# Attention's queries, keys and gates as paired products, and attention's softmax beside branch B's output projection

## The chip, the cores and the metric

One core of a Trainium2 chip runs the whole program. The metric is the device time of one execution in microseconds (us). The kernel before took 1786.78 us, the median of 3 runs (1786.04 to 1786.87).

## The reference

One layer over 512 tokens of width 2048, all in float32. h = RMSNorm(x) goes through one wide projection, whose columns feed two mixers and two merge gates:

```
a_out  = dsa_mixer(aq, ak, av, iq, ik, iw) * silu(az)      # 8 heads x 128, top-k keys by an index score
b_out  = retention_mixer(rope(rq), rope(rk), rv) * silu(rz) # 8 heads x 128, groupnorm
merged = sigmoid(ga) * (a_out @ w_a_out) + sigmoid(gb) * (b_out @ w_b_out)
r      = x + merged @ w_o
out    = rmsnorm(r + (p @ w_ple) * sigmoid(r @ w_ple_gate)) * final_gain
```

Keys that aren't selected get a bias of -1e30 in attention's logits, so attention is computed over all keys up to the query's tile of 128 tokens.

## The kernel before

**Products.** Activations lie transposed: 128 channels on the partitions, 512 tokens along the row. A float32 product is made of three fp32r products: weights and activations are each split in a high part (a ScalarE copy, L137 for weights) and a low part (a subtraction on VectorE or POOL, L143), and TensorE adds high*high, high*low and low*high. `gemm` (L207, matmuls at L197 to L199) does this for one block of 128 output channels: 16 steps over K, three matmuls of 512 columns each.

**Paired products.** `gemm_pair` (L214, matmuls at L249 and L250) makes two output blocks at once from seven half-K products of sums of weight blocks and sums of token halves (a Strassen-like scheme): 7 x 8 steps, each one matmul of 512 and one of 256 columns. It needs the combined inputs `Xh` (56 tiles, made once, kept in DRAM as `hd`, loaded by `x_load`), and its weight sums come from accumulating DMAs on POOL's queue and one VectorE addition (L145). ScalarE copies and VectorE additions (L223, L227, L853) put the outputs together.

**Order.** The order of every engine's instructions is that of the program text. Each K step of a product calls `step()`, which counts a tick and lets side work in: what `later(n, f)` has put n ticks ahead, else the next of the queue `todo`, else, every `rate` ticks, one of the background list `bg`. The background list holds, in this order, the making of `hd`, the top-k rounds on VectorE (L605, L606), and the position bias: four masks on VectorE (L620) and 12 small matmuls (L628) for each of 32 groups, written to `scr` in DRAM. Weights are split 4 units and loaded 9 units ahead of their use, on SP's queue; a unit is 8 K steps of one block.

**Stages.** (1) Index keys and queries with their scores; (2) retention: values (L693 to L695) for four heads, then per head two products `ps_rq` and `ps_rk`, with rotation, scores, states, GroupNorm and a turn back (`turn`, L761) as side work; (3) 22 pairs: branch B's gates, both merge gates and half of attention's gates; (4) branch B's output projection, 16 blocks `ps_w` of 8 steps, with x read again and split in its ticks; (5) attention: values for four heads, then per head the products `ps_aq` and `ps_ak`, and in the ticks of the next head's products the softmax; at its end four more gate products `ps_z` (`gated`); (6) attention's output projection, `ps_w` again from 1327.2 us on; (7) paired products with w_o; (8) the last gate, in 12 blocks and a wider tail.

**Attention of one head.** Logits from split queries and keys (L677 to L679; the first 128 tokens unsplit, L935), added to bias and mask and maximized on VectorE (L937); exponentials with sums on ScalarE (L953); normalization on VectorE (L963, L964); 128 block turns of 32x32 for all heads, 16 a head, on VectorE (`flip`, L708); split into high (L975, ScalarE) and low (L977, VectorE); outputs on TensorE (L989, L991) from split values (L943, L945). The mask is added to the bias on POOL (L916). In this stage and in retention POOL makes the low parts of the weights (`pool_units`).

**Buffers.** 65 slots of 128x512 (`U`), 5 of 128x1280 (`B`), 8 PSUM banks (`P`), 7 raw weight buffers.

Of the kernel before, what the change touches and what calls it, by code (L numbers as in the profile page):

```python
# [34 lines left out]
def block_kernel(tc, xT, pT, posb, posq, w_in, w_v, w_ik, w_a, w_b, w_o, w_ple, w_gate,  # L35
# [4 lines left out]
    with contextlib.ExitStack() as ctx:  # L40
# [265 lines left out]
        for h in range(NH):  # L306
            if h % 4 == 0:
                u_rv.append(block(w_v[h // 4], (2,) * 8, 512))
            if h < NH - 1:
                u_r.append([block(col(g, h), K8) for g in (RQ, RK)])  # L310
            else:
                ids = [block(col(g, h)[:, k:k + 8, :], (8,)) for k in (0, 8) for g in (RQ, RK)]
                u_r.append([ids[0] + ids[2], ids[1] + ids[3]])
        u_rz = [block_pair(col(RZ, h), col(RZ, h + 1)) for h in range(0, NH, 2)]
        u_gb = [block_pair(col(GB, m), col(GB, m + 1)) for m in range(0, 16, 2)]
        u_ga = [block_pair(col(GA, m), col(GA, m + 1)) for m in range(0, 16, 2)]
        u_az = [block_pair(col(AZ, h), col(AZ, h + 1)) for h in range(0, AZ_PAIRED, 2)]
        u_wb = [block(w_b[m], (8,)) for m in range(16)]
        u_a, u_av = [], []
        for h in range(NH):  # L320
            if h % 4 == 0:
                u_av.append(block(w_v[2 + h // 4], (2,) * 8, 512))
            u_a.append([block(col(g, h), K8) for g in (AQ, AK)])
        u_az += [block(col(AZ, h), K8) for h in range(AZ_PAIRED, NH)]
# [5 lines left out]
        pool_units.append((u_a[0][0][0] + 4, u_a[-1][1][-1] + 9))  # L330
# [223 lines left out]
        todo.extend(N3 * 2 + [f_sum] + N3 + [f_rnat] + N3 * 3 + [f_bcast, None, f_keys1] + N3 * 3 + [f_keys2] + N3 * 2 + [f_keys3] + N3 * 2)  # L554
# [127 lines left out]
        def values(ids, name):  # L682
# [3 lines left out]
            for s, (i, k) in enumerate(seq):  # L686
                if k == 0:
                    split_to(i + AHEAD)
                    load_to(i + AHEAD + LOADS)
                h, l = loaded[i]  # L690
                a, b = hparts[s]
                for t in range(NT):
                    pe.matmul(pss[t], a[:, tok(t)], h[:, k], start=(s == 0), stop=False)  # L693
                    pe.matmul(pss[t], a[:, tok(t)], l[:, k], start=False, stop=False)  # L694
                    pe.matmul(pss[t], b[:, tok(t)], h[:, k], start=False, stop=(s == KT - 1))  # L695
                    step()
            vs = [U(name) for _ in range(NT)]
# [4 lines left out]
        def flip(dst, src, n, pairs):  # L702

            d = dst[:, 0:128 * n].rearrange("p (t q) -> p t q", q=128)
            f = src[:, 0:128 * n].rearrange("p (t q) -> p t q", q=128)
            for i in pairs:
                a, b = divmod(i, 4)
                dve.transpose(out=d[32 * a:32 * a + 32, :, 32 * b:32 * b + 32],  # L708
                              in_=f[32 * b:32 * b + 32, :, 32 * a:32 * a + 32])


        yd, bd, zd = (dp.tile([NH, 128, L], F32, name=n) for n in ("yd", "bd", "zd"))
# [11 lines left out]
        def retention_head(h, vs):  # L724
# [4 lines left out]
            if h < NH - 1:  # L729
                pq = gemm(u_r[h][0], hparts, "ps_rq")  # L730
            else:
                i = u_r[h][0][0]
                split_to(i + 4)
                load_to(i + 11)
                x_load(X_AHEAD)
                pq, pk = gemms([(u, slice(0, 128), hparts, ALL, n) for u, n in zip(u_r[h], ("ps_rq", "ps_rk"))],
                               ahead=3, each=lambda s: x_load(2))
            sq = rotate(pq)
            qd = U("qd")
            later(5, lambda: pool.tensor_mul(  # L740
                qd[:, 0:384].rearrange("p (t q) -> p t q", t=3), sq[:, 128:].rearrange("p (t q) -> p t q", t=3),
                dect[:, None, 128:256].to_broadcast([128, 3, 128])))
            if h < NH - 1:
                pk = gemm(u_r[h][1], hparts, "ps_rk")
# [37 lines left out]
            def values_out(t):  # L782
# [6 lines left out]
                if t:  # L789
                    pe.matmul(o, qd[:, tok(t - 1)], E["s"][:, tok(t - 1)], start=False, stop=True)  # L790
# [28 lines left out]
            todo.extend([None] * 5)  # L819
            todo.extend([scores, lambda: keys(0), None, lambda: keys(1)] + [None] * 3 + [states, None, None])  # L820
            todo.extend([lambda t=t: values_out(t) for t in range(NT)])
            todo.extend([None, norm] + [None] * 5 + [scale] + [None] * 5 + [lambda: back(0), None, lambda: back(1)])
# [11 lines left out]
        for h in range(NH):  # L834
            if h % 4 == 0:
                rv = values(u_rv[h // 4], "rv")
            retention_head(h, rv)
        for i in range(len(x_wanted)):
            later(4 + 2 * i, lambda: x_load(1))
        hparts.clear()  # L840
# [5 lines left out]
        def gate_pair(ids, func, finish):  # L846
# [4 lines left out]
            def done(c0, c1, i, q):  # L851
# [3 lines left out]
                if have[i] == 2:  # L855
                    later(1, lambda: (act.activation(o, o, func), finish(i, o)))
# [3 lines left out]
        def to(dst):  # L860
            return lambda i, o: act.dma_start(dst[i], o)

        for n, u in enumerate(u_rz):
            y = B("y2")

            def b_out(i, o, y=y, n=n):
                pool.tensor_mul(o, o, y[:, L * i:L * i + L])
# [7 lines left out]
            gate_pair(u, AF.Silu, b_out)  # L875
        for us, dst in ((u_gb, sgb), (u_ga, sga)):
            for n, u in enumerate(us):
                gate_pair(u, AF.Sigmoid, to(dst[2 * n:2 * n + 2]))
# [6 lines left out]

        for n in range(AZ_PAIRED // 2):
            if n == AZ_PAIRED // 2 - 1:
# [3 lines left out]
            gate_pair(u_az[n], AF.Silu, to(zd[2 * n:2 * n + 2]))  # L891


        def x_again(k):
            xs[k] = U("xk")
            sp.dma_start(xs[k], xT[:, k, :])
            later(5, lambda: x_split(k))

        state["rate"] = 2
        todo.extend([f for k in range(KT) for f in (lambda k=k: x_again(k), None, None, None)])  # L900
        for m in range(16):
            s = U("sg")
            sp.dma_start(s, sgb[m])
            pw = gemm(u_wb[m], bparts, "ps_w")
            dve.tensor_mul(s, pw, s)
            later(4, lambda m=m, s=s: sp.dma_start(mbs[m], s))
        drain()


        oTs = []  # L910

        def attention_head(h, vs):
            hc = slice(128 * (h % 4), 128 * (h % 4) + 128)
            bm = B("bm")
            sp.dma_start(bm, scr[h])
            pool.tensor_add(bm, bm, mneg)  # L916
            ps = gemm(u_a[h][0], hparts, "ps_aq")
            q = U("aq")
            dve.scalar_tensor_tensor(q, ps, 128.0 ** -0.5, R["b"], op0=OP.mult, op1=OP.mult)
            qs = split(q, "aq", 1)  # L920
            ps = gemm(u_a[h][1], hparts, "ps_ak")
            k = U("ak")
            dve.tensor_mul(k, ps, R["b"])
            ks = split(k, "ak", 1)
            mx = S("mx", 4)
            sums = S("sums", 4)
            E = {}

            def logits(t):
                ln = 128 * (t + 1)  # L930
                ps = P("ps_l")
                if t:
                    three(ps[:, :ln], qs, ks, tok(t), slice(0, ln))
                else:
                    pe.matmul(ps[:, :ln], q[:, tok(t)], k[:, 0:ln], start=True, stop=True)  # L935
                lg = bm[:, TOFF[t]:TOFF[t] + ln]
# [3 lines left out]
            def values_split():  # L940
                vh, vl = U("avh", F32R), U("avl", F32R)
                for j in range(NT - 1):
                    act.activation(vh[:, tok(j)], vs[j][:, hc], AF.Copy)  # L943
                for j in range(NT - 1):
                    dve.tensor_sub(vl[:, tok(j)], vs[j][:, hc], vh[:, tok(j)].bitcast(F32))  # L945
                E["v"] = vh, vl

            def exps():
                nm = S("nm", 4)
                dve.tensor_scalar(nm, mx, -1.0, None, op0=OP.mult)  # L950
                for t in range(NT):
                    lg = bm[:, TOFF[t]:TOFF[t] + 128 * (t + 1)]
                    act.activation(lg, lg, AF.Exp, bias=nm[:, t:t + 1], accum_out=sums[:, t:t + 1])  # L953

            def normalize():
                ri = S("ri", 4)
                dve.reciprocal(ri, sums)
                E["pn"] = B("pn")
                pn = E["pn"].rearrange("p (a c) -> p a c", c=128)
                for t in range(NT):  # L960
                    n = min(t + 1, 3)
                    src = bm[:, TOFF[t]:TOFF[t] + 128 * n].rearrange("p (a c) -> p a c", c=128)
                    dve.tensor_scalar(pn[:, t:t + 3 * n - 2:3, :], src, ri[:, t:t + 1], None, op0=OP.mult)  # L963
                dve.tensor_scalar(pn[:, 7, :], bm[:, 1152:1280], ri[:, 3:4], None, op0=OP.mult)  # L964

            def turn(i):
                if i < 8:
                    flip(bm, E["pn"], 10, (2 * i, 2 * i + 1))
                    return
                if i == 8:  # L970
                    E["p"] = B("pth", F32R), B("ptl", F32R)
                pth, ptl = E["p"]
                c = slice(0, 512) if i % 2 == 0 else slice(512, 1280)
                if i < 10:
                    act.activation(pth[:, c], bm[:, c], AF.Copy)  # L975
                else:
                    dve.tensor_sub(ptl[:, c], bm[:, c], pth[:, c].bitcast(F32))  # L977
# [4 lines left out]
            def outs(n):  # L982
# [3 lines left out]
                for i in range(3 * n, min(3 * n + 3, len(seq))):  # L986
                    a, b, j = seq[i]
                    if j == NT - 1:
                        pe.matmul(po[:, 384:], vs[j][:, hc], bm[:, 896:1024], start=False, stop=False)  # L989
# [3 lines left out]
                if n == 3:  # L993
                    oT = U("oT")
                    act.activation(oT, po, AF.Copy)
                    oTs.append(oT)

            todo.extend([None] * 2 + [values_split])
            todo.extend([lambda t=t: logits(t) for t in range(NT)])
            todo.extend([exps] + [None] * 6 + [normalize])  # L1000
            todo.extend([None] + [lambda i=i: turn(i) for i in range(8)] + [None] * 4)
# [365 lines left out]
```

## Time and profile before

| | us |
|---|---|
| median of the runs | 1786.78 |
| profiled execution | 1787.27 |
| its span | 1785.3 |
| TensorE waits that ended on another engine, the three longest groups | 10.4, 6.8, 5.2 |
| stage 2, retention | 104.8 to 404.5 |
| stage 3, 22 pairs | 404.5 to 856.6 |
| stages 4 and 5 | 856.6 to 1327.2 |
| stages 6 to 8 | 1327.2 to 1785.3 |

The profile is of one execution. PE is a matmul on TensorE, PEld a load of its stationary operand, DVE is VectorE, ACT ScalarE, POOL GpSimd, SP the engine that issues most DMAs. A group of instructions has its source line, engine, operation, tiles (out<-in), shapes and count, then busy time and mean nanoseconds of one, then the engine's idle time just before and what ended it. Rows of the timeline begin with the start and the duration in us. A row on one tile has the shortest, median and longest duration, then the first and last start. Matmuls overlap, and their ends are modelled, so the distance between two starts is what a matmul costs TensorE.

### The profile page before, as it was taken

To read this page: it belongs to the slowest core of one execution; us is meant where nothing else is said; L and a number is where in the kernel's file an instruction comes from. 1 tells how busy PE (TensorE), PEld (TensorE's weight loads), DVE (VectorE), ACT (ScalarE), POOL (GpSimd) and SP (SyncE) were. 2 spreads that over 40 slices of the span, in tenths; PEclk is the share of its full clock that TensorE was granted. 3 is DMA by queue.
4 is the path that set the end of the run, shared out by engine and by line. 5 is a ranking of instruction groups with operands and counts; after the bars stand their busy time and mean duration, and the time that the engine had idled before them with its cause. 6 is when DMAs were issued, how large, how long until landed. Compare 5 with 4: busy or idle time off the path is not lost. (4 is left out here: it accounts for less than half of the span.)

```text
span 1785.3 us, 23792 instructions
## 1 busy us (share of the span) xinstructions
PE 1742.2 (98%) x8966; PEld 1463.7 (82%) x8966; DVE 1198.4 (67%) x1929; ACT 762.7 (43%) x1117; POOL 392.6 (22%) x262
## 2 busy tenths in 40 slices
PE   9999999998999999999999999998989999999997
PEld 7988788887888888888776777886778788888887
DVE  7787885777777676777755367457658877774453
ACT  7464232113555555555532333333434444464332
POOL 2002444532321111110000144354310011011222
PEclk9999999999999999999999999999999999999999
DMA  7337753379988888888965432333236588742312
GB/s 284 106 101 257 232 185 112 98 264 294 267 205 207 220 215 209 208 213 210 319 223 170 138 109 75 104 109 118 73 129 202 155 216 210 193 158 97 95 59 95
DMA packets 114579, 309.64 MB, mean 173 GB/s; under 512 B 12832, under 2 KB 21024, under 8 KB 114464
## 3 DMA queue, kind: packets, MB, share of 16 engines
q1 hardware_dynamic: 91072, 244.15, 40.7%
q0 software_dynamic: 13600, 49.29, 15.6%
q10 hardware_dynamic: 9792, 14.68, 2.5%
q8 instruction: 70, 1.15, 0.3%
q14 instruction: 45, 0.37, 0.1%
HBM read 266.14 MB, written 41.94 MB: 173 GB/s over the span
## 5 line engine op out<-in xcount | busy, mean ns | idle before, releaser
L137 ACT ACTIVATE wh<-wraw 128x1024 fp32r<-128x1024 f32 (+2 forms) x404 | 418.9, 1044 | 421.9 <-issue 100.5
L143 DVE TENSOR_TENSOR wl<-wraw,wh 128x1024 fp32r<-128x1024 f32 (+2 forms) x324 | 400.3, 1244 | 219.0 <-ACT wh L137 210.2
L143 POOL TENSOR_TENSOR wl<-wraw,wh 128x1024 fp32r<-128x1024 f32 x80 | 191.9, 2401 | 345.6 <-ACT wh L137 340.1
L105 POOL DMA_DIRECT2D wraw<-w_in x66 | 58.1, 956 | 339.1 <-DVE wl L143 241.6
L249 PE MATMUL ps_p<-hs,wh 128*128 128x512 f32 x352 | 126.6, 399 | 0.0
L693 PE MATMUL ps_vn<-wh,hh 128*128 128x512 f32 x256 | 102.1, 399 | 0.0
L694 PE MATMUL ps_vn<-wl,hh 128*128 128x512 f32 x256 | 100.1, 391 | 0.0
L695 PE MATMUL ps_vn<-wh,hl 128*128 128x512 f32 x256 | 99.9, 390 | 0.0
L250 PE MATMUL ps_p<-hs,wl 128*128 128x256 f32 x352 | 98.8, 281 | 0.0
L223 ACT ACTIVATE e<-ps_p 128x512 f32<-128x512 f32 x90 | 53.8, 597 | 103.7 <-PE ps_p L250 101.4
L249 PEld LDWEIGHTS ps_p<-hs,wh 128*128 128x128 f32 x352 | 66.1, 188 | 16.6
L199 PE MATMUL ps_pg<-rh,wl 128*128 128x512 f32 x192 | 74.7, 389 | 0.0
L197 PE MATMUL ps_pg<-rh,wh 128*128 128x512 f32 x192 | 74.7, 389 | 0.0
L198 PE MATMUL ps_pg<-rl,wh 128*128 128x512 f32 x192 | 74.7, 389 | 0.0
L250 PEld LDWEIGHTS ps_p<-hs,wl 128*128 128x128 f32 x352 | 66.5, 189 | 0.0
L105 POOL DMA_DIRECT2D wraw<-w_o x24 | 21.3, 958 | 203.0 <-DVE wl L143 166.0
L708 DVE STREAM_TRANSPOSE bm<-pn 32x320 f32<-32x320 f32 x128 | 64.4, 503 | 1.9
L249 PE MATMUL ps_p<-ha,wh 128*128 128x512 f32 x176 | 65.5, 409 | 0.0
L249 PE MATMUL ps_r<-hs,wh 128*128 128x512 f32 x176 | 63.8, 401 | 0.0
L249 PE MATMUL ps_v<-hs,wh 128*128 128x512 f32 x176 | 63.7, 401 | 0.0
L249 PE MATMUL ps_q<-ha,wh 128*128 128x512 f32 x176 | 63.7, 401 | 0.0
L249 PE MATMUL ps_v<-ha,wh 128*128 128x512 f32 x176 | 63.4, 400 | 0.0
(390 smaller groups left out, 4673.9 us busy)
## 6 DMA issues: line engine op xcount, KB each, us to landing
wraw<-w_in SPq DMA_DIRECT2D x174, 512.0 KB, 4.6
wraw<-w_in POOLq DMA_DIRECT2D x66, 512.0 KB, 7.9
wraw<-w_v SPq DMA_DIRECT2D x32, 512.0 KB, 4.1
wraw<-w_o SPq DMA_DIRECT2D x32, 512.0 KB, 4.7
wraw<-w_o POOLq DMA_DIRECT2D x24, 512.0 KB, 7.7
wraw<-w_gate SPq DMA_DIRECT2D x24, 512.0 KB, 3.7
hd<-hs SPq DMA_DIRECT2D x32, 256.0 KB, 2.5
hs<-hd SPq DMA_DIRECT2D x32, 256.0 KB, 6.0
```

What stands on the lines that cost most here:

```text
L105: pool.dma_start(out=raw_tiles[r], in_=src[:, k0:k0 + 8, :], accum_op=OP.add)
L137: act.activation(h, raw, AF.Copy)
L143: e.tensor_sub(l, raw, h.bitcast(F32))
L197: pe.matmul(o, h[:, k, w], a, start=(s == order[0]), stop=False)
L198: pe.matmul(o, h[:, k, w], b, start=False, stop=False)
L199: pe.matmul(o, l[:, k, w], a, start=False, stop=(s == order[-1]))
L249: pe.matmul(o, h[:, k], x, start=(n < 4 and k == 0), stop=False, skip_group_check=True)
L250: pe.matmul(o[:, LO], l[:, k], x[:, LO], start=False, stop=(k == 7), skip_group_check=True)
L693: pe.matmul(pss[t], a[:, tok(t)], h[:, k], start=(s == 0), stop=False)
L694: pe.matmul(pss[t], a[:, tok(t)], l[:, k], start=False, stop=False)
L695: pe.matmul(pss[t], b[:, tok(t)], h[:, k], start=False, stop=(s == KT - 1))
L708: dve.transpose(out=d[32 * a:32 * a + 32, :, 32 * b:32 * b + 32], in_=f[32 * b:32 * b + 32, :, 32 * a:32 * a + 32])
```

## The change

- Attention's queries and keys become 8 pairs (query block with key block of one head), and all of its gates 4 pairs instead of 2; the pairs grow from 22 to 32. Queries, keys and values go to DRAM (`qd`, `kd`, `vd`) and come back per head.
- Attention's values are made right after retention's last head, in whose ticks the 56 tiles of `Xh` are loaded; x is not read and split a second time, and head 7's two products are no longer interleaved.
- Attention's softmax and outputs lie in the ticks of branch B's output projection, head h starting at tick 14h (`HEAD`), at fixed ticks through `later` instead of `todo`. No `drain` stands before or after.
- The turned probabilities come from TensorE transposes (10 a head) instead of VectorE's 16 block turns; ScalarE normalizes (it was VectorE), the mask is added on VectorE (it was POOL), and VectorE splits all weights of that stage.
- Retention's side work moves from `todo` to fixed ticks; its first scores are at tick 8 instead of 6 for heads 0 and 4. The first normalization of x (`f_sum`, `f_rnat`) comes 3 and 9 ticks later.
- Background work runs every 4 ticks instead of 3 up to the pairs, and every 10 instead of 24 in them.

```diff
-        u_az = [block_pair(col(AZ, h), col(AZ, h + 1)) for h in range(0, AZ_PAIRED, 2)]
+        u_qk = [block_pair(col(AQ, h), col(AK, h)) for h in range(NH)]
+        u_az = [block_pair(col(AZ, h), col(AZ, h + 1)) for h in range(0, NH, 2)]
...
-        pool_units.append((u_a[0][0][0] + 4, u_a[-1][1][-1] + 9))
...
-        todo.extend(N3 * 2 + [f_sum] + N3 + [f_rnat] + N3 * 3 + [f_bcast, None, f_keys1] + N3 * 3 + [f_keys2] + N3 * 2 + [f_keys3] + N3 * 2)
+        todo.extend(N3 * 3 + [f_sum] + N3 * 3 + [f_rnat] + N3 * 3 + [f_bcast, None, f_keys1] + N3 * 3 + [f_keys2] + N3 * 2 + [f_keys3] + N3 * 2)
...
+            at = (8, 9, 11, 15, 18, 19, 20, 21, 23, 27, 32, 34) if h % 4 == 0 else \
+                (6, 7, 9, 13, 16, 17, 18, 19, 21, 26, 32, 34)
+            for n, f in zip(at, (scores, lambda: keys(0), lambda: keys(1), states,
+                                 *(lambda t=t: values_out(t) for t in range(NT)), norm, scale,
+                                 lambda: back(0), lambda: back(1))):
+                later(n, f)
...
+        for i in range(2):
+            vs = values(u_av[i], "av", lambda s, i=i: x_load(2 * i or s // 4))
+            for t in range(NT):
+                act.dma_start(vd[4 * i + t], vs[t])
...
+        for h in range(NH):
+            def qk_out(i, o, h=h):
+                if i == 0:
+                    act.activation(o, o, AF.Copy, scale=128.0 ** -0.5)
+                act.dma_start((qd, kd)[i][h], o)
+
+            gate_pair(u_qk[h], qk_out)
...
-            pool.tensor_add(bm, bm, mneg)
...
+            def mask():
+                dve.tensor_add(E["bm"], E["bm"], mneg)
...
+                for t in range(NT):
+                    lg = E["bm"][:, TOFF[t]:TOFF[t] + 128 * (t + 1)]
+                    act.activation(lg, lg, AF.Copy, scale=ri[:, t:t + 1])
...
             def turn(i):
-                if i < 8:
-                    flip(bm, E["pn"], 10, (2 * i, 2 * i + 1))
-                    return
+                ps = E["pt", i] = P("ps_pt")
+                js = [(0, t) for t in range(4)] if i == 0 else [(1, 1), (1, 2), (1, 3), (3, 3)] if i == 1 \
+                    else [(2, 2), (2, 3)]
+                for n, (j, t) in enumerate(js):
+                    pe.transpose(ps[:, tok(n)], E["bm"][:, TOFF[t] + 128 * j:TOFF[t] + 128 * j + 128], ident)
...
+            steps = [(-12, loads), (-3, mask), (0, lambda: parts("aq")), (1, lambda: parts("ak"))]
+            steps += [(n, lambda t=t: logits(t)) for t, n in enumerate((4, 5, 6, 7))]
+            steps += [(8, exps), (9, values_split), (13, normalize), (14, lambda: gate(0))]
+            steps += [(n, lambda i=i: turn(i)) for i, n in enumerate((17, 18, 19))]
+            steps += [(n, lambda i=i: high(i)) for i, n in enumerate((18, 19, 20))]
+            steps += [(n, lambda i=i: low(i)) for i, n in enumerate((19, 20, 21))]
+            steps += [(n, lambda n=n: outs(n - 23)) for n in (23, 24, 25, 26)]
+            steps += [(28, lambda: gate(1)), (29, lambda: gate(2))]
...
-BG_RATE = 3
-BG_RATE2 = 24
-X_AHEAD = 10
-AZ_PAIRED = 4
+BG_RATE = 4
+BG_RATE2 = 10
+HEAD = 14
```

More of the change, by code (lines that the diff above doesn't have):

```diff
@@ L700, in values @@
             return vs
[L702 to L712, printed above, removed]
+        yd, bd, zd, qd, kd, vd = (dp.tile([NH, 128, L], F32, name=n) for n in ("yd", "bd", "zd", "qd", "kd", "vd"))
         def rotate(ps):
@@ L993, in outs @@
                 if n == 3:
[L994 to L1001, printed above, removed]
-            todo.extend([lambda i=i: turn(i) for i in range(8, 12)] + [None, None])
@@ L1040, in block_kernel, with project_b @@
+        def project_b(m):
+            s = U("sg")
+            sp.dma_start(s, sgb[m])
+            pw = gemm(u_wb[m], bparts, "ps_w")
+            dve.tensor_mul(s, pw, s)
+            later(4, lambda: sp.dma_start(mbs[m], s))
+        for m in range(16):
+            project_b(m)
         merged = {}
```

191 lines of the change are left out of this document (74 added, 117 removed).

## The prediction

> **What bounds the kernel now.** I read the page's busy times first, then the windows by stage, then what TensorE waited for.
>
> ```profile
> span 1785.3 us, 23792 instructions
> PE 1742.2 (98%) x8966; PEld 1463.7 (82%) x8966; DVE 1198.4 (67%) x1929; ACT 762.7 (43%) x1117; POOL 392.6 (22%) x262
> ```
>
> TensorE is busy for 98% of the span, so what counts is its own issue time plus its few waits. The windows give, for each stretch, its length and the busy time of PE, PEld, DVE, ACT and POOL, then the granted clock, DMA share and GB/s:
>
> ```profile
> 436.80:856.60 419.80, 419.80 (x2461) 361.77 (x2460) 301.73 (x378) 229.39 (x289) 68.55 (x76) 1.00 0.87 223
> 856.60:963.90 107.30, 107.30 (x604) 81.28 (x603) 67.85 (x121) 40.14 (x56) 0.00 (x0) 1.00 0.72 242
> 963.90:1327.10 363.20, 345.52 (x1581) 277.43 (x1580) 208.53 (x374) 124.62 (x212) 130.95 (x55) 0.98 0.32 105
> ```
>
> The paired products (first row) and branch B's projection (second) run with no TensorE idle at all. The attention stage (third: values, query and key products, attention, last gates) has 17.7 us of idle and a clock below 1.00. TensorE's waits (us, times, longest) say on what:
>
> ```profile
> PE ps_o L991 <- ACT pth L975: 10.4, 9, 4.9
> PE ps_o L991 <- DVE ptl L977: 6.8, 6, 4.3
> PE ps_t L761 <- DVE yn L807: 5.2, 1, 5.2
> ...
> PE ps_ms L393 <- DVE sq L448: 2.9, 1, 2.9
> ...
> PE ps_rs L751 <- DVE ra L721: 2.5, 1, 2.5
> ```
>
> The first two are the end of each head's softmax chain (VectorE's turned probabilities, split in two); the third is the tail of retention head 7, which lies in the first pair.
>
> **Issue rates.** A matmul's shown duration has a modelled end, so I price TensorE by the distance of starts.
>
> ```profile
> L197 PE MATMUL ps_w<-ah,wh x128: 389/389/390, 1327.2 to 1413.5; 128*128 128x512 f32 x128
> ```
> ```profile
> 600.83 0.40 PE L249 MATMUL ps_p<-ha,wh 128*128 128x512 f32 x1
> ...
> 604.72 0.40 PE L249 MATMUL ps_q<-ha,wh 128*128 128x512 f32 x1
> ```
>
> 128 plain steps of three matmuls start over 86.3 us: 0.680 us a step. In a pair, 11 steps (512 and 256 columns) lie between the two rows: 3.89/11 = 0.354 us.
>
> **The change, part by part.**
>
> *Products.* Out go 16 query and key products and 4 gate products of 16 plain steps: 20 x 16 x 0.680 = 217.6 us. In come 8 query/key pairs and 2 gate pairs of 56 steps: 10 x 56 x 0.354 = 198.2 us. **-19.4 us.** Other engines must keep that pace: in the pairs' window VectorE is at 301.73/419.80 = 72%, ScalarE at 55%, DMA at 0.87. A background step every 10 steps instead of 24 adds 3.3 a pair, mostly masks of at most 0.48 us (below): 1.3 us of VectorE in 19.8, still under 80%. Without that cover a pair would be late by what VectorE lacks.
>
> ```profile
> L620 DVE TENSOR_SCALAR mk<-relf,thr 128x512 bf16<-128x512 f32 x32 | 13.2, 480 | 0.0
> ```
>
> *Values* move beside retention's end with the same matmuls: 0. The bias matmuls move from attention into the pairs with their issue time: 0. The 56 loads of combined inputs go to SP during the values; each waits for a slot, and behind it on SP are weight loads issued nine units ahead, over 40 us early. Re-reading and splitting x beside branch B's projection goes; that stretch had no PE idle: 0.
>
> *Transposes.* 80 on TensorE, in 24 groups, replace 128 on VectorE.
>
> ```profile
> L761 PE MATMUL ps_t<-cs,ra x24: 270/272/274, 185.4 to 420.1; 128*128 128x128 f32 x24
> ```
> ```profile
> 241.28 0.49 PE L761 MATMUL ps_t<-cs,ra 128*128 128x128 f32 x3
> 241.52 0.48 PE L197 MATMUL ps_rq<-hh,wh 128*128 128x512 f32 x1
> 241.84 0.39 PE L198 MATMUL ps_rq<-hl,wh 128*128 128x512 f32 x1
> ```
>
> Three take 0.24 us, and the matmul behind them 0.32 to its successor instead of 0.23. So 80 x 0.08 + 24 x 0.09 = **+8.6 us**. If each cost its shown 0.272 us instead, it would be 21.8 us; that is a rival below. The Trainium skill (TensorE: Matmul & The Clock Gate, Part 4: PE-mode transpose) speaks for the dearer case: it gives about 275 ns for a transpose in a kernel, and says that transposes don't raise the clock gate as matmuls do. The shown duration agrees with it; the pitch of the starts, which is what TensorE pays here, does not.
>
> *Waits that go.* The 17.7 us of idle in attention, 0.16 us more for each of some 17 waits (modelled end 0.39 against a pitch of 0.23), and slow matmuls after the longest waits:
>
> ```profile
> 415.44 0.63 PE L249 MATMUL ps_p<-ha,wh 128*128 128x512 f32 x1
> ...
> 418.00 0.63 PE L249 MATMUL ps_p<-ha,wh 128*128 128x512 f32 x1
> ```
>
> Four steps in 2.56 us are 0.64 each, not 0.354: after a 5.2 us wait TensorE ran at about half rate for some eight steps, 2.3 us. Three such spots of some 1.2 us in attention (whose window has a clock of 0.98) make it 17.7 + 2.7 + 3.6 = **-24 us**. The tail of head 7 (5.2 + 2.3 = **-7.5 us**) goes because its steps now count values' 0.680 us, not a pair's 0.354: VectorE gets twice the time. Summing the squares moves 3 steps and its use 9 steps later, in steps of 384 columns, 0.680 x 384/512 = 0.51 us: 4.6 us more time, **-2.9 us**. Head 0's scores go from step 6 to 8: 1.4 of 2.5 us, **-1.4 us**. Together -19.4 + 8.6 - 24 - 7.5 - 2.9 - 1.4 = **-46.6 us**.
>
> *Waits that come.* Attention no longer has 300 us of products to hide behind, but 16 blocks of branch B's projection: 128 steps, 14 a head. TensorE's own work per head is 14 x 0.680 = 9.5 us, logits and outputs 27 half-widths x 0.114 = 3.1 us, transposes 1.1 us: 13.7 us. The first transposes wait for the normalized probabilities, and the whole projection queues behind them. I walk the ring from one head's last logits to the next's, in the new order on VectorE and ScalarE, with these prices:
>
> ```profile
> 1039.05 0.40 ACT L953 ACTIVATE bm<-bm,nm 128x128 f32<-128x128 f32 x1
> ...
> 1041.16 0.19 ACT L953 ACTIVATION_READ_ACCUMULATOR bm<-bm,nm 128x1 f32 x1
> ```
> ```profile
> 1033.48 0.68 DVE L945 TENSOR_TENSOR avl<-av,avh 128x128 fp32r<-128x128 f32 x3
> ```
> ```profile
> L143 DVE TENSOR_TENSOR wl<-wraw,wh 128x1024 fp32r<-128x1024 f32 x311 | 390.9, 1264 | 213.8 <-ACT wh L137 205.2 <-PE ps_q L250 8.3
> L905 DVE TENSOR_TENSOR sg<-ps_w,sg 128x512 f32<-128x512 f32 x16 | 11.0, 688 | 21.8 <-PE ps_w L199 21.8
> L673 DVE TENSOR_TENSOR bl<-bk,bh 128x512 fp32r<-128x512 f32 x8 | 5.5, 690 | 2.0 <-ACT bh L672 2.0
> L937 DVE CUSTOM_DVE_ANT_0 bm<-ps_l,bm 128x512 f32<-128x512 f32 x8 | 5.5, 686 | 3.0 <-PE ps_l L679 3.0
> L816 ACT ACTIVATE yT<-ps_t,g_sb 128x512 f32<-128x512 f32 x8 | 5.5, 684 | 4.7 <-PE ps_t L761 4.7
> L672 ACT ACTIVATE bh<-bk 128x512 fp32r<-128x512 f32 x8 | 5.0, 625 | 3.3 <-DMA bk<-bd 2.9 <-ACT go L856 0.4
> ```
>
> Negated maxima 0.2; four exponentials 2.3; VectorE stands meanwhile, since its next work, the split of the values, waits for ScalarE copies queued behind the exponentials: first copy 0.3, split 0.7; then on VectorE product 0.7, mask add 1.6 (1.264 x 1280/1024; it was on POOL), weight split 1.3, reciprocal 0.2; four scaled copies on ScalarE about 2.0 (0.68 for the widest); high part of the queries 0.6; three splits 2.1; and, laced with the next head's logits, four maxima, three splits of turned probabilities, a product and a second weight split: 0.3 + 0.7 + 0.7 + 0.4 + 1.3 + 0.5 + 0.5 + 0.4 + 0.8 = 5.6. In all 17.6 us. Neighbours on one engine overlap by some 0.07 (three value splits take 0.68, not 3 x 0.28), about 1.2, and a head has 1.75 weight splits, not two: 16 us. So TensorE waits about 2.2 us a head, at the first transposes, 7 times: 15 us.
>
> From below: VectorE's own work alone is about 11.5 us a head, under 13.7, so if the order let it run ahead there would be no wait. From above: 17.6 us with every handover charged, 4 us a head, or 28 us. I take 15, near the walk.
>
> *The first head* has nothing ahead of it. Its loads are issued as the projection starts:
>
> ```profile
> bm<-scr SPq DMA_DIRECT2D x8, 640.0 KB, 5.2
> ```
>
> Landing 5.2, mask 1.6, two splits 1.4: 8.2 us, against five steps (3.4 us) and a start some 1 us early on SP: 4 us late; then its chain with a table load for the exponential ends some 4 us after the transposes are due: 8 to 9 us. I add 2 us for half-rate matmuls behind these waits. **+26 us** in all.
>
> Sum: -46.6 + 26 = -20.6 us. The profiled execution took 1787.27 us (span 1785.3 and 2.0 around it), so 1766.7; that is 0.5 above the median of 1786.78, so I predict **1766**.
>
> **Rivals.**
>
> *TensorE sets the pace after all.* VectorE idle at 28% in all stages speaks for it, the value split waiting behind the exponentials against. Only the first head's wait remains, 5 to 9 us: 1745 to 1749.
>
> *The softmax ring decides (slower).* If VectorE and ScalarE alternate with longer handovers, the ring sets the whole projection. Break-even: 26 becomes 46.6, that is, (46.6 - 11)/7 = 5.1 us a head, a ring of 18.8 us. At 20.3 us, 15% above the full-duration walk, and with TensorE falling to half rate once a head (1.2 us as above), it costs 11 + 7 x 7.8 = 66 us: 1806. For it: today's heads have their worst waits (4.9, 4.3) where chains meet. Against: VectorE's slowest splits fell beside POOL's, and POOL has nothing to do in that stage.
>
> ```profile
> L673 DVE TENSOR_TENSOR aql<-aq,aqh 128x512 fp32r<-128x512 f32 x8 | 16.9, 2110 | 6.1 <-ACT aqh L672 6.1
> ```
>
> *Pairs don't hold 0.354.* DMA already has a share of 0.87 there. If 32 pairs lose 0.4 us each, 13 us: 1779. Against: the window shows no idle in 419.80 us.
>
> *The transposes cost their shown duration* (21.8 instead of 8.6 us): 1779. For it: a group must finish before its copies start. Against: the pitch above, with other matmuls right behind. By the skill's rule on transposes it would come out here.
>
> **How the numbers follow.** Forecast 0.50, TensorE's pace 0.25, ring 0.12, pairs 0.08, transposes 0.05. A measurement of this kernel tells about 0.2% (3.6 us) from no change. Faster takes all but the ring, less 0.05 for the edges of the other cases that come within 0.2%: 0.83; same 0.05; slower 0.12. The range reaches from the low rival (1744) to where the ring nearly eats the gain (1788).
>
> **What would show it.** Right: 32 pairs at 19.8 us; a projection stretch near 147 us (87 + 8 x 4.2 + 26) with TensorE waiting on the scaled copies at the first transpose of each head; no wait at head 7's turn back. Wrong: waits there over 5 us a head, idle between pairs, transposes further apart than 0.11 us, or SP loads landing late in the projection.

## The result, and the profile after

The changed kernel took **1746.27 us**, the median of 4 runs (1743.90 to 1748.32), beside 1786.41 (1785.91 to 1786.87) for the kernel before on the same chip: a ratio of 0.9775, 95% interval 0.9758 to 0.9792, or 40.1 us less. The forecast was 1766: the sign held, the range only just (its low end was 1744), and the gain was twice as large as predicted. The profiled execution took 1746.99 us.

The page's busy times and, below them, TensorE's longest waits (us, times, longest), both of the kernel after:

```profile
span 1745.1 us, 24500 instructions
PE 1719.9 (99%) x9206; PEld 1459.5 (84%) x9206; DVE 1206.4 (69%) x1909; ACT 819.4 (47%) x1224; POOL 287.8 (16%) x236
```
```profile
PE ps_l L667 <- ACT akh L662: 3.9, 1, 3.9
PE ps_b L1222 <- POOL rl L1218: 3.7, 1, 3.7
PE ps_pt L953 <- ACT bm L944: 3.6, 11, 1.3
PE ps_v L249 <- DVE ms L265: 2.8, 1, 2.8
```

The three groups of before that the prediction spoke of (10.4 and 6.8 at attention's outputs, 5.2 at a turn back) are gone; 3.9 at the first head's logits and 3.6 at the transposes have come. The 3.7 and 2.8 lie in the stages that the change does not touch.

The windows by stage, of before and then of after (length; busy time of PE, PEld, DVE, ACT and POOL; granted clock, DMA share, GB/s). The rows are the index stage; retention (after: with attention's values); the pairs; then projection and attention; then all that follows. The first pair and a part of the second lie in before's second row.

```profile
0.00:104.90 104.90, 99.58 (x526) 90.07 (x527) 81.49 (x136) 63.10 (x102) 17.25 (x15) 0.97 0.55 184
104.90:436.80 331.90, 324.14 (x1582) 271.80 (x1581) 243.00 (x501) 108.20 (x172) 109.42 (x58) 0.99 0.59 193
436.80:856.80 420.00, 420.00 (x2462) 361.93 (x2461) 301.93 (x378) 229.59 (x290) 68.55 (x76) 1.00 0.87 223
856.80:1327.20 470.40, 452.72 (x2183) 358.60 (x2182) 276.18 (x494) 164.56 (x268) 130.95 (x55) 0.98 0.41 136
1327.20:1785.30 458.10, 445.76 (x2221) 381.31 (x2219) 295.82 (x423) 197.20 (x288) 66.43 (x58) 0.99 0.53 150
```
```profile
0.00:96.90 96.90, 94.17 (x515) 85.55 (x516) 78.48 (x130) 60.44 (x96) 17.24 (x15) 1.00 0.58 199
96.90:488.80 391.90, 391.90 (x1913) 326.75 (x1912) 260.36 (x533) 123.70 (x193) 106.94 (x56) 1.00 0.55 181
488.80:1144.10 655.30, 654.57 (x3922) 554.98 (x3921) 474.97 (x616) 352.41 (x444) 98.40 (x108) 1.00 0.85 220
1144.20:1287.80 143.60, 134.76 (x642) 109.88 (x641) 97.50 (x210) 87.28 (x207) 0.00 (x0) 0.96 0.64 222
1287.80:1745.10 457.30, 444.44 (x2221) 382.22 (x2219) 294.94 (x423) 195.43 (x286) 65.21 (x57) 0.99 0.54 152
```

Read length minus PE for the idle time, and length times what the clock lacks for the slow time. After, retention and values have neither, the pairs 0.7 us of idle; of what is left, the change has to do with the part in the 143.6 us of projection and attention: 8.8 us of idle and 0.04 x 143.6 = 5.7 us of missing clock. The last stage, with 12.9 us of idle after and 12.3 before, is nearly the same in both.

### The profile page after: what moved, and what is told of

Same layout as the page of the kernel before. It is cut to its first block, busy times and chain, and to the rows that moved or that the text cites. A ratio compares the mean times of both kernels' runs of the same rounds, so it can differ in the third digit from the quotient of the medians.

```text
span 1745.1 us, 24500 instructions
## 1 busy us (share of the span) xinstructions
PE 1719.9 (99%) x9206; PEld 1459.5 (84%) x9206; DVE 1206.4 (69%) x1909; ACT 819.4 (47%) x1224; POOL 287.8 (16%) x236
## 4 chain that ended last, share of the span: by engine, by line
PE 92%; DVE 4%; ACT 2%; DMA 1%; issue 0%; SPq 0%; POOL 0%; DVEq 0%; ACTq 0%
PE ps_p L249 13%; PE ps_v L249 8%; PE ps_p L250 6%; PE ps_q L249 4%; PE ps_r L249 4%; PE ps_v L250 4%; PE ps_vn L683 3%; PE ps_vn L684 3%; PE ps_vn L685 3%; PE ps_pg L198 2%; PE ps_pg L197 2%; PE ps_pg L199 2%; PE ps_w L199 2%; PE ps_w L198 2%; PE ps_w L197 2%; PE ps_q L250 2%
## 5 line engine op out<-in xcount | busy, mean ns | idle before, releaser
L143 DVE TENSOR_TENSOR wl<-wraw,wh 128x1024 fp32r<-128x1024 f32 (+2 forms) x398 | 488.6, 1234 | 268.2 <-ACT wh L137 264.2
L137 ACT ACTIVATE wh<-wraw 128x1024 fp32r<-128x1024 f32 (+2 forms) x434 | 449.8, 1045 | 399.1 <-issue 77.0
L249 PE MATMUL ps_p<-hs,wh 128*128 128x512 f32 x512 | 185.0, 401 | 0.7 <-ACT e L223 0.7
L250 PE MATMUL ps_p<-hs,wl 128*128 128x256 f32 x512 | 143.8, 281 | 0.0
L223 ACT ACTIVATE e<-ps_p 128x512 f32<-128x512 f32 x120 | 71.8, 598 | 131.2 <-PE ps_p L250 125.4
L249 PEld LDWEIGHTS ps_p<-hs,wh 128*128 128x128 f32 x512 | 96.2, 188 | 27.1 <-issue 2.3
L143 POOL TENSOR_TENSOR wl<-wraw,wh 128x1024 fp32r<-128x1024 f32 x36 | 86.4, 2401 | 189.4 <-ACT wh L137 189.2
L250 PEld LDWEIGHTS ps_p<-hs,wl 128*128 128x128 f32 x512 | 96.7, 189 | 0.0
L249 PE MATMUL ps_v<-ha,wh 128*128 128x512 f32 x256 | 92.6, 401 | 0.0
L249 PE MATMUL ps_v<-hs,wh 128*128 128x512 f32 x256 | 92.5, 400 | 0.0
L250 PE MATMUL ps_v<-hs,wl 128*128 128x256 f32 x256 | 71.9, 281 | 0.0
```

Of the source, the lines that this page charges most:

```text
L137: act.activation(h, raw, AF.Copy)
L143: e.tensor_sub(l, raw, h.bitcast(F32))
L223: act.activation(E[n], src, AF.Copy)
L249: pe.matmul(o, h[:, k], x, start=(n < 4 and k == 0), stop=False, skip_group_check=True)
L250: pe.matmul(o[:, LO], l[:, k], x[:, LO], start=False, stop=(k == 7), skip_group_check=True)
```

## The experiments

Two theories were set against each other. **Turns and ring**: the gain comes from taking the turns off VectorE; what the new arrangement costs is a ring of VectorE and ScalarE that is longer than TensorE's own work per head. **TensorE's pace**: there is no ring left, TensorE's work sets the time, and only the first head waits. Times are medians, ratios are to the kernel before beside the same runs; the medians of before varied from 1786.4 to 1790.0 between batches, so ratios are the safer comparison. The kernel after was run only in the first batch; where an edit of it gains little, the lengths of its stages in the profile say more than a difference of medians.

### Only the turns, in the kernel before

```diff
-                if i < 8:
-                    flip(bm, E["pn"], 10, (2 * i, 2 * i + 1))
-                    return
+                ps = E["pt", i] = P("ps_pt")
...
+                    pe.transpose(ps[:, tok(n)], bm[:, TOFF[t] + 128 * j:TOFF[t] + 128 * j + 128], ident)
```

> The kernel before, with only the turn of the probabilities moved to TensorE transposes (10 a head). Theory (turns): attention's waits before, 17.2 us idle before the outputs and some 25 us with half-rate matmuls, came from VectorE's 16 block turns a head (8 us). Without them nearly all of it goes and the transposes add 7 us: 15 to 20 us faster, about 1768 us, waits of the outputs under 4 us. Rival (place): the waits come from where attention lay, in the ticks of the next head's products, and of which the turns are no cause: the waits stay, the transposes add 7 us, about 1793 us.

Measured: 1772.32 us, ratio 0.991 (0.9893 to 0.9928), span 1769.3, 16.0 less than before. Its TensorE waits:

```profile
PE ps_t L761 <- DVE yn L807: 5.2, 1, 5.2
...
PE ps_ms L393 <- DVE sq L448: 2.9, 1, 2.9
...
PE ps_rs L751 <- DVE ra L721: 2.5, 1, 2.5
PE ps_l L678 <- DVE akl L673: 2.0, 8, 0.3
```

The 17.2 us at the outputs have gone but for 0.6, the three waits of the other stages stand. The edit has some of the turns' surroundings in it as well: the probabilities are normalized in place and split straight from PSUM, in fewer steps. The prediction's -24 (waits) and +8.6 (transposes), together -15.4, are right as a pair.

### The turns back on VectorE, in the kernel after

The mask, the loading of the bias and the steps behind the turns are shifted with them.

```diff
-                    pe.transpose(ps[:, tok(n)], E["bm"][:, TOFF[t] + 128 * j:TOFF[t] + 128 * j + 128], ident)
+                    dve.transpose(out=d[32 * a:32 * a + 32, :, 32 * b:32 * b + 32],
+                                  in_=f[32 * b:32 * b + 32, :, 32 * a:32 * a + 32])
...
-            steps += [(n, lambda i=i: turn(i)) for i, n in enumerate((17, 18, 19))]
+            steps += [(14 + i, lambda i=i: turn(i)) for i in range(8)]
```

> The changed kernel, with the turn of the probabilities back on VectorE (16 block turns a head, 8 us), and its later ticks shifted for them. Theory (turns): VectorE's own work rises from about 11 to 19 us a head, above TensorE's 14.5, and VectorE becomes the bound of branch B's projection: its stretch grows from 143.6 us by 35 to 50 us, 1781 to 1796 us. Rival (place): the ring had slack in its new place, only the 7 us of transposes go: 1738 to 1746 us.

Measured: 1840.23 us, ratio 1.0285 (1.0267 to 1.0302). The stretch of projection and attention, in its window:

```profile
1144.00:1379.00 235.00, 160.22 (x557) 123.97 (x556) 163.72 (x336) 87.18 (x206) 0.00 (x0) 0.80 0.40 136
```
```profile
L959 DVE STREAM_TRANSPOSE bm<-pn 32x320 f32<-32x320 f32 x128 | 64.3, 503 | 37.6 <-ACT pn L951 35.6
```

235 us instead of 143.6, TensorE idle for 75 and at a clock of 0.80. With 64.3 us of block turns on VectorE (second row) in series with the rest, a head takes some 29 us. That is the rival "the softmax ring decides" in pure form: without the transposes on TensorE this new arrangement is slower than before. It cost twice what I expected. VectorE itself is busy for only 163.7 of the 235 us, so the order of the steps, which were shifted and not fitted, has a share in it; how large a share this run doesn't show.

### The first head's work earlier

```diff
...
+                heads = [attention_head(h) for h in range(NH)]
+                for t, (_, f) in zip((28, 44, 49, 50), heads[0][:4]):
+                    later(t, f)
+            gate_pair(u_az[n], to(zd[2 * n:2 * n + 2], AF.Silu))
...
```

> The changed kernel, with the first head's loads, mask and splits put 28, 12, 7 and 6 ticks before the end of the last gate pair instead of at the projection's start. Theory: the wait of the first logits (3.9 + 0.8 + 0.4 us idle, then matmuls at half rate, 8 to 9 us in all) goes and nothing else moves: 1737 to 1739 us. Rival (ring): the later heads keep their distance through VectorE and ScalarE, so what the first head gains is waited for at the transposes: 1743 to 1747 us, with the waits of the transposes longer by as much.

Measured: 1750.28 us, ratio 0.9786 (0.977 to 0.9802): no gain. The wait moved. A row of its TensorE waits, and one of ScalarE's timeline:

```profile
PE ps_p L249 <- ACT e L223: 6.5, 1, 6.5
```
```profile
1144.20 0.63 ACT L662 ACTIVATE bh<-bk 128x512 fp32r<-128x512 f32 x1 [5.93 <-DMA bk<-bd]
```

The early loads went ahead of branch B's on SP, ScalarE stood 5.93 us for one of those, and the pair's own copies (L223) stood behind it. This settled neither theory.

### The old places of the first normalization

```diff
-        todo.extend(N3 * 3 + [f_sum] + N3 * 3 + [f_rnat] + N3 * 3 + [f_bcast, None, f_keys1] + N3 * 3 + [f_keys2] + N3 * 2 + [f_keys3] + N3 * 2)
+        todo.extend(N3 * 2 + [f_sum] + N3 + [f_rnat] + N3 * 3 + [f_bcast, None, f_keys1] + N3 * 3 + [f_keys2] + N3 * 2 + [f_keys3] + N3 * 2)
```

> The changed kernel, with the old places of the sum of squares and its use (3 and 9 ticks earlier). Theory: the wait of 2.9 us comes back, with some 2 us of slower matmuls around it: 1749 to 1752 us, the index stage longer by 6 to 8 us of which 2 us (11 scores) only move. Rival: the shorter stage only moved work into retention, and all of it comes back there: 1746 to 1747 us.

Measured: 1751.76 us, ratio 0.9794 (0.9779 to 0.9809), span 1749.2. The first and last starts of one matmul of the pairs, in the kernel after and in this one:

```profile
L249 PE MATMUL ps_v<-hs,wh x256: 389/398/499, 488.9 to 1125.9; 128*128 128x512 f32 x128
```
```profile
L249 PE MATMUL ps_v<-hs,wh x256: 389/398/499, 494.9 to 1131.8; 128*128 128x512 f32 x128
```

The pairs begin 6.0 us later. The wait itself is 2.9; the other half is the slow time behind it (the clock of 0.97 in before's first window, 3.1 us), which the prediction didn't price here.

### The mask on GpSimd

```diff
-                dve.tensor_add(E["bm"], E["bm"], mneg)
+                pool.tensor_add(E["bm"], E["bm"], mneg)
...
-            steps = [(-12, loads), (-3, mask), (0, lambda: parts("aq")), (1, lambda: parts("ak"))]
+            steps = [(-12, loads), (-4, mask), (0, lambda: parts("aq")), (1, lambda: parts("ak"))]
```

> The kernel after, with the mask of each head (128x1280, 1.48 us on VectorE) added by GpSimd, one tick earlier. Theory A (the ring of VectorE and ScalarE still costs TensorE about 1 us a head): the ring of a later head gets 1.5 us shorter, the distance between the first transposes of two heads falls from some 15.3 to some 14.5 us, and the projection stretch from 143.6 to some 138 us: 3 to 6 us faster than after. Theory B (TensorE's own work sets the pace of the heads, 14.5 us): the distance stays, the stretch stays within 1.5 us, and the time within 2 us of after. If the longer GpSimd addition becomes a wait of its own, the splits of the queries and keys are late and the waits of the logits grow: slower.

Measured: 1749.58 us, ratio 0.978 (0.9759 to 0.9801): no faster than after. Two rows of its timeline, on POOL and on VectorE, and TensorE's wait that follows:

```profile
1233.72 2.82 POOL L908 TENSOR_TENSOR bm<-bm,mneg 128x1280 f32<-128x1280 f32 x1 [14.55 <-PE ps_pt L953]
```
```profile
1233.97 3.11 DVE L663 TENSOR_TENSOR akl<-ak,akh 128x512 fp32r<-128x512 f32 x1
```
```profile
1237.14 0.39 PE L668 MATMUL ps_l<-akl,aqh 128*128 128x256 f32 x1 [2.16 <-DVE akl L663]
```

A split that takes 0.68 us alone took 3.11 beside GpSimd's addition: it ended at 1237.08, 0.54 us after the addition did (1236.54). So VectorE gained 1.5 us and lost 2.4. The Trainium skill (SBUF — State Buffer, "Who interferes with whom") says that a VectorE instruction with two inputs in SBUF contends with a GpSimd instruction that reads SBUF, and that the lock on the ports they share is exclusive. The trace agrees: 3.11 us instead of 0.68. TensorE's waits for that split came to 6.8 us in this kernel (0.8 in after). As a test of the ring this run is spoilt by it.

### The split of the values behind the normalization

```diff
-            steps += [(8, exps), (9, values_split), (13, normalize), (14, lambda: gate(0))]
+            steps += [(8, exps), (13, normalize), (16, values_split), (14, lambda: gate(0))]
```

> The kernel after, with the split of the values moved behind the normalization (tick 16 instead of 9), so that VectorE no longer stands 2.9 us behind the exponentials. Theory A (ring): VectorE gains up to 2.9 us a head ahead of the mask and the splits, the distance of the heads falls to some 14.5 us, 3 to 6 us faster than after. Theory B (TensorE's own work sets the pace): within 2 us of after, and only VectorE's idle time moves.

Measured: **1740.54 us**, ratio 0.9725 (0.9706 to 0.9743), some 6 us faster than after by the medians; the stretch shrank from 143.6 to 138.2. Two heads' first transposes, of after and of this kernel:

```profile
1184.53 0.70 PE L953 MATMUL ps_pt<-cs,bm 128*128 128x128 f32 x3
...
1199.57 0.49 PE L953 MATMUL ps_pt<-cs,bm 128*128 128x128 f32 x3
```
```profile
1182.21 0.60 PE L953 MATMUL ps_pt<-cs,bm 128*128 128x128 f32 x4
...
1196.54 0.60 PE L953 MATMUL ps_pt<-cs,bm 128*128 128x128 f32 x4
```

In this kernel no matmul waits between the two rows, so 14.33 us is TensorE's own work for a head; four of the seven distances are 14.3. In the kernel after the distances are 17.2, 15.0, 14.8, 15.3, 15.9, 15.6 and 14.8, on average 15.5. The first of them, 17.2, is the same in both kernels and isn't the ring: behind the first head's transposes, which wait 1.31 us in the kernel after, TensorE ran at half rate once more. Two starts of after, 0.42 us apart instead of 0.23:

```profile
1171.59 0.63 PE L198 MATMUL ps_w<-bl,wh 128*128 128x512 f32 x1
1172.01 0.63 PE L199 MATMUL ps_w<-bh,wl 128*128 128x512 f32 x1
```

The other six are 15.2 on average. So the ring was real, and cost 0.9 us a head, 5.5 in all; of these the edit took away 4.1. VectorE's stand shows in after's timeline of this engine:

```profile
1207.66 0.17 DVE L934 TENSOR_SCALAR nm<-mx 128x4 f32<-128x4 f32 x1
1210.39 0.70 DVE L929 TENSOR_TENSOR avl<-av,avh 128x128 fp32r<-128x128 f32 x3 [2.56 <-ACT avh L927]
1211.01 1.48 DVE L908 TENSOR_TENSOR bm<-bm,mneg 128x1280 f32<-128x1280 f32 x1
```

### All heads four ticks later

```diff
-                later(max(n + HEAD * h, 0), f)
+                later(max(n + HEAD * h + 4, 0), f)
```

> The kernel after, with all steps of all heads 4 ticks (2.7 us) later against the projection. Theory A (the first head is late by a backlog of fixed length on ScalarE and VectorE): its wait of 3.9 us at the logits shrinks to some 1 us and the slow matmuls behind it go with it, 3 to 6 us faster than after, unless the last head, which now ends 4 ticks nearer to the end of the projection, sticks out behind it. Theory B (the first head's chain is bound to the end of the last pair's work in any case, and what comes later is only moved): within 2 us of after, the wait moving to the first transposes.

Measured: 1743.75 us, ratio 0.9745 (0.9724 to 0.9766), span 1739.2 against after's 1745.1. The first head's wait fell to

```profile
PE ps_l L667 <- ACT akh L662: 2.6, 1, 2.6
```

and the wait of 1.3 us at its first transposes is gone; the first two heads lie 15.6 us apart instead of 17.2. By the medians the gain is 2.5 us, by the ratios 5.4, by the spans 5.9, and the stretch of projection and attention is 139.1 us, 4.5 less. So theory A fits, although the wait stays longer than the 1 us I expected. What is late in the kernel after is ScalarE, busy with the last gate pair (timeline of ScalarE, after):

```profile
1148.28 0.62 ACT L662 ACTIVATE aqh<-aq 128x512 fp32r<-128x512 f32 x1
1148.80 1.04 ACT L137 ACTIVATE wh<-wraw 128x1024 fp32r<-128x1024 f32 x1
1150.77 0.63 ACT L841 ACTIVATE go<-go 128x512 f32<-128x512 f32 x1 [0.93 <-DVE go L832]
...
1151.80 0.63 ACT L662 ACTIVATE akh<-ak 128x512 fp32r<-128x512 f32 x1 [0.40 <-ACT go L841]
```

The queries' high part was made at 1148.28; the keys' stands behind the pair's last gate (L841), and that waited for VectorE. It is not the landing of a load, as I had predicted.

### Two tries at the turn back, in the kernel before

The first gives head 7's turn back 16 steps more, the second lets head 6 scale its output three steps earlier:

```diff
-            todo.extend([None, norm] + [None] * 5 + [scale] + [None] * 5 + [lambda: back(0), None, lambda: back(1)])
+            todo.extend([None, norm] + [None] * 5 + [scale] + [None] * (21 if h == NH - 1 else 5) + [lambda: back(0), None, lambda: back(1)])
```

> The kernel before, with the turn back of retention head 7 alone 16 steps later in the first pair (16 x 0.354 = 5.7 us). Theory (the wait of 5.2 us and the half-rate matmuls behind it, 2.3 us, are one late chain that only needs time): the wait falls to under 1 us and the kernel is 5 to 7.5 us faster than before, a ratio of .996 to .997. Rival (the wait is for a resource that the pair takes, VectorE, or the later gates move along with it): the wait stays or moves to another place, ratio 1.000 within .001.

```diff
-            todo.extend([None, norm] + [None] * 5 + [scale] + [None] * 5 + [lambda: back(0), None, lambda: back(1)])
+            todo.extend([None, norm] + [None] * (2 if h == NH - 2 else 5) + [scale]
+                        + [None] * (8 if h == NH - 2 else 5) + [lambda: back(0), None, lambda: back(1)])
```

> The kernel before; for retention head 6 alone the scaling of its output (four instructions on VectorE, 1.36 us) is issued three steps earlier, so that it stands ahead of head 7's eight rotation instructions (5.5 us) and two weight splits (2.35 us) in VectorE's order. Theory (head 6's turn back waits 5.2 us because of that order, and TensorE runs slowly behind the wait): the wait falls below 0.5 us and the slow matmuls go, 5 to 7.5 us faster than before, ratio .996 to .997. Rival (VectorE is the bound at that place and the wait only moves to the next user of VectorE): ratio 1.000 within .001, with a new wait of several us in the first pair.

Measured: 1789.25 us, ratio 1.0003 (0.9991 to 1.0015), and 1789.37 us, ratio 0.9997 (0.9985 to 1.0008). The first left the wait of 5.2 us where it was: I had named the wrong head. Two turns back lie in the first pair, and the one that waits is head 6's, whose scaling stands on VectorE behind head 7's rotations and two weight splits (VectorE's timeline, before):

```profile
408.95 0.69 DVE L721 TENSOR_TENSOR ra<-ra,rb 128x512 f32<-128x512 f32 x1
409.56 2.35 DVE L143 TENSOR_TENSOR wl<-wraw,wh 128x1024 fp32r<-128x1024 f32 x2
411.83 1.36 DVE L807 TENSOR_SCALAR yn<-ps_y,gmv,grs 128x128 f32<-128x128 f32 x4
```

The second took that wait away, and two others came (TensorE's timeline in the second kernel):

```profile
414.54 0.94 PE L774 MATMUL ps_kv<-rv,kn 128*128 128x128 f32 x6 [1.89 <-ACT kn L769]
...
421.59 0.76 PE L790 MATMUL ps_y<-state,qd 128*128 128x128 f32 x2 [4.26 <-ACT state L776]
```

6.2 us in place of 5.2: in the pair's faster steps head 7's chain is late as well. The rival held. Of the things tried, only slower steps for the whole tail, as the change has them with the values, removed the waits; its second window shows no idle at all.

### Both gains together

```diff
-            steps += [(8, exps), (9, values_split), (13, normalize), (14, lambda: gate(0))]
+            steps += [(8, exps), (13, normalize), (16, values_split), (14, lambda: gate(0))]
...
-                later(max(n + HEAD * h, 0), f)
+                later(max(n + HEAD * h + 4, 0), f)
```

> The kernel after with both edits that helped: the split of the values behind the normalization, and all heads 4 ticks later. If they act on two separate costs (the ring of the later heads, and the first head's backlog), their gains add: some 5.7 us and 3.0 us in the medians, 1737 to 1738, ratio about .971. If both only removed the first head's wait, it stays at the better of the two, 1740 to 1741, ratio .9725.

Measured: **1738.31 us**, the median of 4 runs, ratio 0.9708 (0.9688 to 0.9729), the fastest version here. Its stretch of projection and attention:

```profile
1143.00:1276.60 133.60, 129.21 (x642) 107.66 (x641) 96.08 (x209) 85.24 (x206) 0.00 (x0) 0.99 0.68 240
```

143.6 - 5.4 (values) - 4.5 (four ticks, a stretch of 139.1) = 133.7: the two costs were separate and their gains add.

### Every transpose twice

On the kernel with the later split of the values, where TensorE sets the pace of most heads:

```diff
-                for n, (j, t) in enumerate(js):
+                for n, (j, t) in list(enumerate(js)) * 2:
```

> The kernel after with the split of the values behind the normalization, where TensorE's own work sets the pace of the heads (14.3 us), and each of the 80 transposes of attention issued twice, the second writing the same values to the same place. If a transpose costs TensorE the distance of starts (0.08 to 0.11 us), the projection stretch grows by 6 to 9 us and the distance of two heads from 14.3 to some 15.2 us. If it costs its shown duration (0.272 us), by some 22 us and to 17 us; the clock granted in that stretch would be lower too if transposes don't count for it as matmuls do.

Measured: 1747.12 us, ratio 0.9759 (0.9738 to 0.978). The windows of the stretch without and with the doubling, and the latter's later heads:

```profile
1143.20:1281.40 138.20, 132.15 (x643) 109.63 (x642) 97.38 (x210) 86.71 (x208) 0.00 (x0) 0.96 0.68 233
```
```profile
1143.80:1290.30 146.50, 140.71 (x723) 118.62 (x722) 98.64 (x210) 86.96 (x208) 0.00 (x0) 0.97 0.62 220
1184.40:1277.30 92.90, 92.86 (x505) 79.56 (x504) 64.99 (x146) 59.76 (x149) 0.00 (x0) 1.00 0.57 204
```

80 more transposes add 8.3 us: 0.104 us each, near the distance of starts and not the shown 0.272. Five of the seven distances between heads are 15.4 us where they were 14.33 at the least, 0.11 us a transpose. The Trainium skill (TensorE: Matmul & The Clock Gate, Part 4: PE-mode transpose) gives about 275 ns for one; an estimate from that is 22 us for the 80, and the run decides for the pitch. In the window of the later heads (second row) 120 of the 505 matmuls are transposes, and the granted clock is 1.00; there are other matmuls between them, so whether transposes alone would hold it is not shown.

## Why the prediction was right in sign and wrong in size

| term | predicted | measured | from |
|---|---|---|---|
| products | -19.4 | -19.7 | step of 0.353 us, below |
| transposes | +8.6 | +8.3 | doubling |
| waits that go in attention | -24 | about -26 | the turns alone |
| retention's tail and first scores | -8.9 | -11.1 | second windows |
| index stage | -2.9 | -6.0 | old places |
| ring | +15 | +5.5 | 6 x (15.24 - 14.33) |
| first head, half rate | +11 | +12.6 | rest of the stretch |
| sum | -20.6 | about -36 | measured in all: -40.1 |

**Products: right.** In the kernel after, six steps of a pair:

```profile
599.86 0.40 PE L249 MATMUL ps_r<-hs,wh 128*128 128x512 f32 x1
...
601.98 0.40 PE L249 MATMUL ps_r<-hs,wh 128*128 128x512 f32 x1
```

2.12/6 = 0.353 us, so 10 x 56 x 0.353 = 197.9 against 217.6. With 0.7 us of idle in 655.3, the rival "pairs don't hold 0.354" is out.

**Transposes and the waits at the outputs: right.** The turns alone shortened before's stretch from 470.4 to 455.6 us: 14.8 less, although the transposes cost 8.3, so 23.1 of waiting went, and the 2.6 us that remained there went with the full change.

**Waits that come: the step that failed.** The prediction set TensorE's own work of 13.7 us a head against a ring of 16, and took the difference of some 2.2 us for the wait. The ring is there, but as walked it was too long (15.2 measured), and TensorE's own work was taken too small (14.33). The difference of two large numbers carries both errors: 0.8 and 0.6 us a head turned 2.2 into 0.9. The stretch splits as 128 x 0.680 = 87.0, 8 x (14.33 - 14 x 0.680) = 38.5, and 18.1 of waiting and half rate, where the prediction had 26; less 5.5 of ring, 12.6 belong to the first head. That is near the 11 put there, but its cause was misjudged: ScalarE's and VectorE's backlog from the last pair, and half-rate matmuls, more of them than I allowed (last section). That the stretch of 143.6 us came near the 147 of the prediction is luck in part: the waits were 7.9 us less, TensorE's own work 4.9 more.

**Index stage: the size failed.** Half rate behind the wait was left out. Of the 8.0 us by which the stage is shorter, the other 2 are index scores that moved into retention.

**Retention's tail: right in mechanism, wrong in place.** It was head 6, not head 7; the idle (7.8) and slow (3.3) time of before's second window is all gone, so the 2.5 us at the first scores went whole, not 1.4 of them.

**The rivals.** The time fell on "TensorE sets the pace after all" (1745 to 1749), but by luck: its claim, that only the first head waits, doesn't hold. The ring still cost 5.5 us, the later split of the values won back 4.1 of them, and the first head cost 12.6 where that rival had 5 to 9. Other gains, larger than I put them, made up for it. "The softmax ring decides" is what happens if the turns stay on VectorE.

**Open.** About 4 us of the 40.1 are in none of these rows; 0.8 of them lie in the last stage. The clocks of the windows are rounded to 0.01, which is 2.4 us either way over attention's 470. None of my runs separates them.

## What to carry to other kernels

Where two chains run beside each other, the cost is the difference of two lengths: measure both, for errors of 5 and 4% here made it less than half of what was predicted. An engine in a ring that stands behind another engine's queue is the first thing to reorder: one line moved from tick 9 to 16 won 6 us. Taking away a single wait of a late chain only passed it on here; giving the whole chain time removed it.

## What the hardware showed unexpectedly

After the longer waits TensorE ran at about half rate for a while, at times for longer than the wait itself. In the kernel after, behind the first head's 3.9 us (timeline of TensorE, and the window around it):

```profile
1156.23 0.63 PE L197 MATMUL ps_w<-bh,wh 128*128 128x512 f32 x1
1156.65 0.63 PE L198 MATMUL ps_w<-bl,wh 128*128 128x512 f32 x1
...
1159.21 0.41 PE L198 MATMUL ps_w<-bl,wh 128*128 128x512 f32 x1
1159.46 0.39 PE L199 MATMUL ps_w<-bh,wl 128*128 128x512 f32 x1
```
```profile
1152.00:1160.00 8.00, 7.19 (x20) 5.79 (x21) 4.54 (x14) 1.75 (x3) 0.00 (x0) 0.57 0.91 324
```

Starts lie 0.42 us apart instead of 0.23 from the end of the wait (1152.48) to 1159.2, 6.7 us at half rate, which costs 3.2 us beside the wait's 3.9. With waits of 2.4 and 0.9 us, in the fastest kernel, it lasted from 1154.3 to 1157.7, 3.4 us. Behind the first head's transposes, which waited 1.3 us in the kernel after and 0.7 with the values split later, it lasted some 3 us; with heads 4 ticks later the longest wait there is 0.3 us, and the half rate stays away. So waits of 2.9 and 3.9 us counted about double, that of 5.2 us (2.3 behind it) half as much again. How short a wait has to be to cost nothing behind it, and whether the transposes have a part in it, no run here separates.

Beyond that: a VectorE subtraction on SBUF lasts until GpSimd's addition is through (3.11 us instead of 0.68), so work moved from VectorE to GpSimd can cost VectorE more than it takes off.
